# Hybrid decoder step on one Trainium2 core: the upper and lower parts of the weights made by DMAs

## The chip, the cores and the metric

The kernel runs on one core of a Trainium2 chip. The metric is the device time of one execution in microseconds. Five engines with instruction queues of their own share the work: TensorE (PE in the profile), VectorE (DVE), ScalarE (ACT), GpSimd (POOL) and SyncE (SP, which here only issues DMAs). Each engine takes its instructions in the order of its queue and waits on semaphores for the others.

## The reference

One layer of a decoder is applied to 512 prompt rows and 8 sample rows together (520 columns), in float32:

```
z  = RMSNorm(x) @ w_in              # 1024 -> 10240: q k v g | u v | two merge gates
A  = retention(q, k, v), 4 heads, chunks of 128, per-head RMSNorm, silu(g) * o, @ w_ret_o
B  = u * (tril(W_s[g]) @ LN(v) + b[g]), @ w_gm_o
x  = x + (sigmoid(a_ret) * A + sigmoid(a_gm) * B) @ w_o
x  = x + (silu(f_gate) * f_up) @ w_ffn_down      # f = RMSNorm(x) @ w_ffn_in, hidden 2816
y  = RMSNorm(x)
```

Outputs are y for both groups, the retention states of both and the normalised gMLP rows of the samples. Nearly all of the arithmetic is in the six weight matrices.

## The kernel before

**A float32 product in three passes.** Activations lie transposed in SBUF, features on the 128 partitions and the 520 rows as columns, in two halves of 260. A float32 operand is kept as two float32r parts: an upper part, the rounded value, and a lower part, the remainder. A product is upper x upper + upper x lower + lower x upper, summed in PSUM (`product`, L99). One weight block is 128 output features by up to 1024 input features, 512 KB; it gives 8 x 3 x 2 = 48 matmuls of 260 columns.

**Where the weight parts come from.** `weights` (L84) is called once for each block, 180 times in a run: 80 for `w_in`, 16 for `w_ret_o`, 8 each for `w_gm_o` and `w_o`, 44 for `w_ffn_in`, 24 for `w_ffn_down` (8 of them with 768 input features; three are kept for the last tile). SP loads the block into `wraw` (three buffers), ACT copies it to the float32r tile `whi`, which rounds, and DVE subtracts `whi` from `wraw` into `wlo` (`split`, L76). `whi` and `wlo` have two buffers each. The first two blocks come in pieces (`cuts`), so that PE can start on the first piece.

**Stages.** After a start in which x is loaded and split, four heads follow (q, k, v, gate, scores, output, state; the output projection `ps_ro` of a head runs within the next one), then the gMLP branch with the merge gates, then `w_gm_o`, `w_o`, the 44 blocks of the FFN's first matrix and the 24 of its second. In the heads each of 8 samples per head has a state of 512 KB that SP loads (`S`), DVE updates and POOL stores (`out_rss`, L444); POOL also broadcasts the samples' q and k (`qkb`, L436) from a small store in DRAM (`qks`).

**What sets the order.** The program is written in the order of the mathematics; a scheduler of the language reorders the instructions of every engine by its own timeline, and waits follow from the tiles' buffers. POOL does some elementwise work (`sq`, `qf`, `kf`, `gt`, `br`, `gu`, `ms`, `fa`) and issues a few DMAs; its queue, like the others, is in order: an instruction that waits holds up all that stand behind it.

Of the kernel before, what the change touches and what calls it, by code (L numbers as in the profile page):

```python
# [7 lines left out]
F32 = mybir.dt.float32  # L8
F32R = mybir.dt.float32r
I32 = mybir.dt.int32  # L10
AF = mybir.ActivationFunctionType
ALU = mybir.AluOpType

P = 128
# [27 lines left out]
def step_kernel(ctx: ExitStack, tc: tile.TileContext, io):  # L42
    nc = tc.nc

    const = ctx.enter_context(tc.tile_pool(name="const", bufs=1))
    wp = ctx.enter_context(tc.tile_pool(name="wp", bufs=2))
    big = ctx.enter_context(tc.tile_pool(name="big", bufs=NBIG))
    tmp = ctx.enter_context(tc.tile_pool(name="tmp", bufs=NTMP))
    small = ctx.enter_context(tc.tile_pool(name="small", bufs=3))
# [5 lines left out]
    def ttile(name):  # L55
        return tmp.tile([P, T], F32, name=name, tag="tmp")
# [4 lines left out]
    def wide(name, dt=F32):  # L61
        return big.tile([P, 2, T], dt, name=name, tag="big")

    def flat(t):
        return t.rearrange("p a b -> p (a b)")[:, 0:D]
# [10 lines left out]
    def split(hi, lo, src, hi_eng=None, lo_eng=None):  # L76

        if hi_eng is None:
            nc.scalar.copy(out=hi, in_=src)  # L79
        else:  # L80
            hi_eng.tensor_copy(out=hi, in_=src)
        (lo_eng or nc.vector).tensor_tensor(out=lo, in0=src, in1=hi.bitcast(F32), op=ALU.subtract)  # L82

    def weights(src, n, cuts=(), keep=False):  # L84

        raw = wp.tile([P, 8 * P], F32, name="wraw", tag="wraw", bufs=3)
        if keep:
            hi, lo = flat(wide("khi", F32R)), flat(wide("klo", F32R))
        else:
            hi = wp.tile([P, 8 * P], F32R, name="whi", tag="whi")  # L90
            lo = wp.tile([P, 8 * P], F32R, name="wlo", tag="wlo")
        at = [0, *cuts, n]
        for a, b in zip(at, at[1:]):
            sl = slice(a * P, b * P)
            nc.sync.dma_start(out=raw[:, sl], in_=src[:, sl])
            split(hi[:, sl], lo[:, sl], raw[:, sl])
        return hi, lo

    def product(ps, w, at, x, first, last, fs=(0, 1)):  # L99
# [112 lines left out]
    def z_tile(m, name, w=None):  # L212
        w = w or weights(io["w_in"][m], KT)
        ps = acc_psum(name)
        for kt in range(KT):
            product(ps, w, kt, xg[kt], kt == 0, kt == KT - 1)
        return ps
# [7 lines left out]
    rsqrt_table(ones_f)  # L225
    x_load(0)
    w_first = [weights(io["w_in"][0], KT, (2, 4))]
    x_split(0)
    x_load(1)
    x_load(2)  # L230
    x_split(1)
    x_split(2)
    w_first.append(weights(io["w_in"][1], KT, (4,)))
    for kt in range(3, KT):
        x_load(kt)
# [468 lines left out]
    for i in range(KT):  # L704
# [6 lines left out]
        hi = hs[:, i, :]  # L711
# [16 lines left out]
    a = None  # L728
    for i in range(NF):
        a, b = ttile("fa"), ttile("fb")  # L730
# [34 lines left out]
    for i in range(KT - 1):  # L765
        ps = acc_psum("ps_fd")
        down(ps, down_weights(i))
        hi = hs[:, i, :]
# [7 lines left out]
    hi = hs[:, i, :]  # L776
    ps = [aux(f"ps_fd{f}") for f in range(2)]
    blocks = list(down_weights(i, keep=True))
    for f in range(2):
# [5 lines left out]
        if f == 1:  # L785
# [8 lines left out]
            out=hi[:, cols], in0=hi[:, cols], scalar=gains[:, 2, i : i + 1], in1=r, op0=ALU.mult, op1=ALU.mult  # L794
# [5 lines left out]
        for ks in (slice(0, 4), slice(4, 6), slice(6, 8)):  # L800
            nc.sync.dma_start(
                out=io["yT"].rearrange("(k p) t -> p k t", p=P)[:, ks, cols], in_=hs[:, ks, cols]
# [72 lines left out]
```

## Time and profile before

| | |
|---|---|
| time, median of 2 runs | 1162.28 us (1161.21 to 1163.35) |
| profiled execution, its time | 1165.98 us |
| its span, first to last instruction | 1164.2 us |
| PE, PEld busy | 98%, 97% of the span |
| DVE, ACT, POOL busy | 57%, 37%, 18% |
| HBM read, written | 125.02 MB, 21.10 MB |

Busy shares are means over stages; PEld is the load of the stationary operand, which overlaps with PE. The clock that was granted to TensorE is given as a share of 2.4 GHz (1.00 is full speed). DMAs issued from SP stand in the hardware queue, those issued from POOL in the software queue; both use the same 16 DMA engines.

### The profile page before, as it was taken

Reading aid. Unit: us, or ns where it says so; the run is one execution under the profiler, and the core shown is the slowest. Engines: PE = TensorE matmul, PEld = TensorE weight load, DVE = VectorE, ACT = ScalarE, POOL = GpSimd, SP = SyncE. Lnnn points to the kernel's source line nnn. Section 1 sums busy time; section 2 is a strip of 40 time slices with the busy share of each in tenths; the row PEclk is TensorE's granted clock in tenths of the full one; section 3 lists DMA queues with packets and bytes.
Section 4 is the critical chain, followed back from the end, with each engine's and each line's share of the span. In section 5 each row is a group of like instructions: output and inputs, shape, how many; then the busy total and the mean of one; then the engine's idle time right before and its main releaser. Section 6 shows DMA issues by size and latency. Waiting matters only on the chain.

```text
span 1164.2 us, 21641 instructions
## 1 busy us (share of the span) xinstructions
PE 1142.0 (98%) x9242; PEld 1125.6 (97%) x9242; DVE 668.8 (57%) x1040; ACT 435.8 (37%) x672; POOL 209.8 (18%) x175
## 2 busy tenths in 40 slices
PE   8999999999999999999999999999999999999995
PEld 7999999999999998999999999999999999999995
DVE  7788738885787589538434456445545454532233
ACT  4366345433653365323223432343222232322220
POOL 7213201420141013002111222211101010101101
PEclk9999999999999999999999999999999999999998
DMA  7267336633763284222222223422232222223222
GB/s 266 86 217 286 110 110 237 244 109 117 261 212 127 74 276 162 73 91 74 90 74 73 91 91 117 139 94 92 88 106 81 104 90 93 87 90 97 86 78 74
DMA packets 44928, 147.53 MB, mean 127 GB/s; under 512 B 5360, under 2 KB 7808, under 8 KB 44824
## 3 DMA queue, kind: packets, MB, share of 16 engines
q1 hardware_dynamic: 37152, 118.76, 30.2%
q0 software_dynamic: 7680, 27.38, 6.4%
q8 instruction: 73, 1.20, 0.4%
q14 instruction: 23, 0.19, 0.0%
HBM read 125.02 MB, written 21.10 MB: 126 GB/s over the span
## 4 chain that ended last, share of the span: by engine, by line
PE 84%; DVE 7%; DMA 3%; ACT 3%; issue 2%; POOL 0%; DVEq 0%; ACTq 0%; POOLq 0%; SPq 0%
PE ps_fg L105 11%; PE ps_fu L105 11%; PE ps_fd L105 10%; PE ps_ro L105 8%; PE ps_v L105 6%; PE ps_ar L105 4%; PE ps_gm L105 4%; PE ps_g L105 4%; PE ps_gu L105 4%; PE ps_wo L105 4%; PE ps_gv L105 4%; PE ps_ag L105 3%; PE k L105 3%; PE q L105 2%; PE ps_o L460 1%
## 5 line engine op out<-in xcount | busy, mean ns | idle before, releaser
L79 ACT CAST whi<-wraw 128x1024 fp32r<-128x1024 f32 (+2 forms) x180 | 184.8, 1027 | 484.9 <-issue 96.3
L82 DVE TENSOR_TENSOR wlo<-wraw,whi 128x1024 fp32r<-128x1024 f32 (+2 forms) x180 | 256.4, 1425 | 99.2 <-ACT whi L79 94.4
L105 PE MATMUL ps_fg<-hg,whi 128*128 128x260 f32 x704 | 112.5, 282 | 0.0
L105 PE MATMUL ps_fu<-hg,whi 128*128 128x260 f32 x704 | 112.5, 282 | 0.0
L105 PE MATMUL ps_fd<-act,whi 128*128 128x260 f32 x616 | 98.8, 282 | 0.0
L105 PEld LDWEIGHTS ps_fg<-hg,whi 128*128 128x128 f32 x704 | 96.2, 188 | 0.0
L105 PEld LDWEIGHTS ps_fu<-hg,whi 128*128 128x128 f32 x704 | 96.2, 188 | 0.0
L105 PEld LDWEIGHTS ps_fd<-act,whi 128*128 128x128 f32 x616 | 84.4, 188 | 0.0
L105 PE MATMUL ps_g<-xg,whi 128*128 128x260 f32 x512 | 82.7, 283 | 0.0
L105 PE MATMUL ps_ro<-gated,whi 128*128 128x260 f32 x512 | 82.6, 283 | 0.0
L105 PE MATMUL ps_v<-xg,whi 128*128 128x260 f32 x512 | 82.3, 282 | 0.0
L105 PEld LDWEIGHTS ps_ro<-gated,whi 128*128 128x128 f32 x512 | 70.6, 188 | 0.7 <-issue 0.2
L105 PE MATMUL ps_fu<-hg,wlo 128*128 128x260 f32 x352 | 70.8, 282 | 0.0
L105 PE MATMUL ps_fg<-hg,wlo 128*128 128x260 f32 x352 | 70.8, 282 | 0.0
L105 PEld LDWEIGHTS ps_v<-xg,whi 128*128 128x128 f32 x512 | 70.1, 188 | 0.0
L105 PEld LDWEIGHTS ps_g<-xg,whi 128*128 128x128 f32 x512 | 69.9, 188 | 0.0
L746 POOL TENSOR_TENSOR fa<-fa,fb 128x520 f32<-128x520 f32 x22 | 28.8, 1308 | 227.6 <-ACT whi L79 192.8
L442 ACT ACTIVATE kv<-qkb,vs 128x256 f32<-128x256 f32 x128 | 54.1, 498 | 26.9 <-DMA qkb<-qks 23.9
L105 PE MATMUL ps_fd<-act,wlo 128*128 128x260 f32 x308 | 61.8, 282 | 0.0
L745 DVE TENSOR_TENSOR fb<-ps_fu,rstd 128x520 f32<-128x520 f32 x21 | 14.7, 700 | 75.1 <-PE ps_fu L105 75.1
L163 POOL TENSOR_TENSOR sq<-sq,sqr 128x520 f32<-128x520 f32 x19 | 32.9, 1732 | 132.7 <-ACT sqr L161 128.4
L447 DVE SCALAR_TENSOR_TENSOR junk<-S,qkb 128x256 f32<-128x256 f32 x128 | 54.0, 422 | 2.3
(250 smaller groups left out, 2509.3 us busy)
## 6 DMA issues: line engine op xcount, KB each, us to landing
wraw<-in_w_in SPq DMA_DIRECT2D x78, 512.0 KB, 3.5
wraw<-in_w_ffn_in SPq DMA_DIRECT2D x44, 512.0 KB, 3.5
S<-in_st SPq DMA_DIRECT2D x32, 512.0 KB, 4.4
out_rss<-S POOLq DMA_DIRECT2D x32, 512.0 KB, 4.6
qkb<-qks POOLq DMA_DIRECT2D x16, 512.0 KB, 5.0
wraw<-in_w_ret_o SPq DMA_DIRECT2D x16, 512.0 KB, 3.5
wraw<-in_w_ffn_down SPq DMA_DIRECT2D x16, 512.0 KB, 3.5
wraw<-in_w_gm_o SPq DMA_DIRECT2D x8, 512.0 KB, 3.5
```

Of the source, the lines that this page charges most:

```text
L79: nc.scalar.copy(out=hi, in_=src)
L82: (lo_eng or nc.vector).tensor_tensor(out=lo, in0=src, in1=hi.bitcast(F32), op=ALU.subtract)
L105: nc.tensor.matmul((ps[f] if isinstance(ps, list) else ps[:, f])[:, 0:HT], a, x[:, k, f * HT : (f + 1) * HT], start=first and n == 0, stop ...
L163: (add or nc.gpsimd).tensor_tensor(out=acc, in0=acc, in1=q, op=ALU.add)
L442: nc.scalar.activation(out=kv[:, j, :], in_=kb, func=AF.Copy, scale=vs[:, j, b : b + 1])
L447: nc.vector.scalar_tensor_tensor(out=junk, in0=S[:, j, :], scalar=1.0, in1=qb, op0=ALU.mult, op1=ALU.mult, accum_out=os_[:, j, b : b + 1],)
L460: nc.tensor.matmul(ps[:, s * P : NP], vtile(s, l)[:, j * P : (j + 1) * P], score(s, k), start=i == 0, stop=i == 11,)
L745: nc.vector.tensor_tensor(out=halves(b), in0=pu, in1=halves(rstd), op=ALU.mult)
L746: nc.gpsimd.tensor_tensor(out=a, in0=a, in1=b, op=ALU.mult)
```

## The change

`weights` no longer loads a plain copy, except for the first two blocks, which keep the old way with one `wraw` buffer. For the other 178 blocks POOL issues a DMA that writes the block into the float32r tile `whi`, rounding on the way. ACT then writes `-whi` into `wlo`. A second DMA from POOL reads the block from DRAM again and adds it to what stands in `wlo`. `whi` and `wlo` have three buffers each in place of two. Line numbers after this place grow by 7.

```diff
-    wp = ctx.enter_context(tc.tile_pool(name="wp", bufs=2))
+    wp = ctx.enter_context(tc.tile_pool(name="wp", bufs=3))
...
-        raw = wp.tile([P, 8 * P], F32, name="wraw", tag="wraw", bufs=3)
         if keep:
             hi, lo = flat(wide("khi", F32R)), flat(wide("klo", F32R))
         else:
             hi = wp.tile([P, 8 * P], F32R, name="whi", tag="whi")
             lo = wp.tile([P, 8 * P], F32R, name="wlo", tag="wlo")
-        at = [0, *cuts, n]
-        for a, b in zip(at, at[1:]):
-            sl = slice(a * P, b * P)
-            nc.sync.dma_start(out=raw[:, sl], in_=src[:, sl])
-            split(hi[:, sl], lo[:, sl], raw[:, sl])
+        if cuts:
+            raw = wp.tile([P, 8 * P], F32, name="wraw", tag="wraw", bufs=1)
+            at = [0, *cuts, n]
+            for a, b in zip(at, at[1:]):
+                sl = slice(a * P, b * P)
+                nc.sync.dma_start(out=raw[:, sl], in_=src[:, sl])
+                split(hi[:, sl], lo[:, sl], raw[:, sl])
+            return hi, lo
+
+        sl = slice(0, n * P)
+        nc.gpsimd.dma_start(out=hi[:, sl], in_=src[:, sl])
+        nc.scalar.activation(out=lo[:, sl], in_=hi[:, sl].bitcast(F32), func=AF.Copy, scale=-1.0)
+        nc.gpsimd.dma_start(out=lo[:, sl], in_=src[:, sl], accum_op=ALU.add)
         return hi, lo
```

The order of POOL's queue changes in three places. First the start of the program, before the change: squares of x (`sqr`), their sum (`sq`), then the rotary step of head 0.

```order
L159 TENSOR_TENSOR sq<-xt 128x520
L159 TENSOR_TENSOR sqr<-xt 128x520 x2
L163 TENSOR_TENSOR sq<-sq,sqr 128x520
L159 TENSOR_TENSOR sqr<-xt 128x520 x2
L163 TENSOR_TENSOR sq<-sq,sqr 128x520
L159 TENSOR_TENSOR sqr<-xt 128x520
L163 TENSOR_TENSOR sq<-sq,sqr 128x520 x5
L276 TENSOR_TENSOR qf<-rs,rc 128x520
```

And with the change, from the last square on; `whi` is the rounding DMA of a block, `wlo` the adding one.

```order
L166 TENSOR_TENSOR sqr<-xt 128x520
L101 DMA whi<-in_w_in 128x1024 x2
L170 TENSOR_TENSOR sq<-sq,sqr 128x520
L101 DMA whi<-in_w_in 128x1024
L170 TENSOR_TENSOR sq<-sq,sqr 128x520 x2
L103 DMA wlo<-in_w_in 128x1024
L170 TENSOR_TENSOR sq<-sq,sqr 128x520
```

The third block's rounding DMA stands behind the sixth square, and its adding DMA behind three more sums. On ACT its negation stands behind the copy of the second product:

```order
L266 COPY qraw<-q_206 128x520
L168 ACTIVATE sqr<-xt 128x520 x2
L266 COPY qraw<-q_256 128x520
L102 ACTIVATE wlo<-whi 128x1024 x3
L79 CAST sqh<-sq 128x520
```

Second place: POOL in a head (the second one), before. Only the samples' DMAs and elementwise work stand here.

```order
L276 TENSOR_TENSOR kf<-rs,rc 128x520
L275 TENSOR_TENSOR kf<-rc,rs 128x520
L403 DMA qks_199<-row 4x8x128
L436 DMA qkb<-qks_199 128x1024 x2
L444 DMA out_rss<-S 128x1024 x3
L436 DMA qkb<-qks_199 128x1024
L444 DMA out_rss<-S 128x1024
L436 DMA qkb<-qks_199 128x1024
```

With the change, in the same head, from the first stores of states on:

```order
L451 DMA out_rss<-S 128x1024 x2
L101 DMA whi<-in_w_in 128x1024
L103 DMA wlo<-in_w_in 128x1024
L451 DMA out_rss<-S 128x1024
L443 DMA qkb<-qks_199 128x1024
L103 DMA wlo<-in_w_in 128x1024
L451 DMA out_rss<-S 128x1024
L101 DMA whi<-in_w_in 128x1024
L443 DMA qkb<-qks_199 128x1024
L451 DMA out_rss<-S 128x1024 x2
L103 DMA wlo<-in_w_in 128x1024
```

Weight DMAs now stand between the samples' DMAs, behind stores that wait for DVE.

Third place: POOL from `w_gm_o` to the end, before.

```order
L695 TENSOR_TENSOR ms<-ms,br_1929 128x520 x2
L163 TENSOR_TENSOR sq<-sq,sqr 128x520 x6
L746 TENSOR_TENSOR fa<-fa,fb 128x520 x22
L163 TENSOR_TENSOR sq<-sq,sqr 128x520 x6
L799 TENSOR_TENSOR hs<-hs,r_12702 128x260 x3
```

With the change, three blocks in the FFN's first matrix, with what each instruction waits for (DMASW: an earlier DMA of POOL's).

```order
L101 DMA whi<-in_w_ffn_in 128x1024 [waits DMASW2_49,PE_49]
L101 DMA whi<-in_w_ffn_in 128x1024 [waits DMASW3_49,PE_49]
L103 DMA wlo<-in_w_ffn_in 128x1024 [waits DMASW4_49,Activation_49]
L753 TENSOR_TENSOR fa<-fa,fb 128x520 [waits DVE_49,Pool_49]
L103 DMA wlo<-in_w_ffn_in 128x1024 [waits DMASW5_49,Activation_49]
L101 DMA whi<-in_w_ffn_in 128x1024 [waits DMASW6_49,PE_49]
L103 DMA wlo<-in_w_ffn_in 128x1024 [waits DMASW7_49,Activation_49]
```

The rounding DMA of a block waits for PE, which must have finished the block three before it; the adding DMA waits for ACT.

## Rows read from the trace of the kernel before

**Rows 1.** The page's first lines: span, busy time of each engine.

```profile
span 1164.2 us, 21641 instructions
PE 1142.0 (98%) x9242; PEld 1125.6 (97%) x9242; DVE 668.8 (57%) x1040; ACT 435.8 (37%) x672; POOL 209.8 (18%) x175
```

**Rows 2.** Chain that ended last, in order of time: start, length, what.

```profile
217.52 11.46 PE q L105 x96
...
330.08 11.46 PE q L105 x96
...
577.11 2.63 PE ps_mix L631 x24
579.73 11.51 PE ps_ar L105 x96
591.25 11.46 PE ps_ag L105 x96
...
632.80 46.01 PE ps_gu L105 x384
...
817.00 5.73 PE ps_fg L105 x48
822.72 5.73 PE ps_fu L105 x48
```

**Rows 3.** Table by stretch: its length, busy us per engine, granted clock, DMA share, GB/s.

```profile
core 0: us, PE busy (x) PEld busy (x) DVE busy (x) ACT busy (x) POOL busy (x), PEclk, DMA share, GB/s
45.00:128.00 83.00, 82.68 (x646) 80.23 (x645) 72.69 (x147) 43.71 (x82) 25.79 (x24) 1.00 0.57 200
...
217.00:330.00 113.00, 113.00 (x898) 110.61 (x897) 84.28 (x165) 52.76 (x93) 21.59 (x22) 1.00 0.51 179
...
770.00:1023.00 253.00, 253.00 (x2123) 253.00 (x2123) 124.95 (x117) 77.71 (x96) 27.48 (x21) 1.00 0.27 92
```

**Rows 4.** Waits of SP's DMA queue: waiter, releaser, us in total, times, longest.

```profile
SPq L95 <- DVE wlo L82: 777.5, 146, 10.0
```

**Rows 5.** Groups by form: busy us, mean ns of one, idle before and its releasers.

```profile
L82 DVE TENSOR_TENSOR wlo<-wraw,whi 128x1024 fp32r<-128x1024 f32 x168 | 244.9, 1458 | 71.7 <-ACT whi L79 66.9
L79 ACT CAST whi<-wraw 128x1024 fp32r<-128x1024 f32 x168 | 176.3, 1049 | 464.5 <-issue 96.3 <-PE ps_fu L105 86.2 <-PE ps_fg L105 54.7
...
L746 POOL TENSOR_TENSOR fa<-fa,fb 128x520 f32<-128x520 f32 x22 | 28.8, 1308 | 227.6 <-ACT whi L79 192.8 <-ACT fa L742 20.2 <-issue 10.1
L515 POOL TENSOR_TENSOR gt<-gt,of 128x520 f32<-128x520 f32 x16 | 26.6, 1691 | 12.6 <-DVE of L501 12.6
```

**Rows 6.** DMA issues: queue, count, KB each, median us from issue to landing.

```profile
wraw<-in_w_ffn_in SPq DMA_DIRECT2D x44, 512.0 KB, 3.5
out_rss<-S POOLq DMA_DIRECT2D x32, 512.0 KB, 4.6
qkb<-qks POOLq DMA_DIRECT2D x16, 512.0 KB, 5.0
out_rsp<-sf POOLq DMA_DIRECT2D x4, 512.0 KB, 3.2
```

**Rows 7.** Line 444, the states' stores: duration min/median/max, wait before, landing.

```profile
L444 POOL DMA_DIRECT2D out_rss<-S x32: 531/531/538, 73.1 to 440.3; - x32
...
  DVE S L443: 186.8, 32
...
DMA to landing us min/median/max: 2.9/4.6/7.2
```

**Rows 8.** Tile qkb, the samples' broadcasts: landing.

```profile
DMA to landing us min/median/max: 4.0/5.0/6.5
```

**Rows 9.** Timeline of the start: start, length, engine, what.

```profile
16.90 1.51 POOL L159 TENSOR_TENSOR sqr<-xt 128x520 f32<-128x520 f32 x1
...
26.11 0.51 PE L105 MATMUL k<-xg,wlo 128*128 128x260 f32 x2 [0.16 <-DVE wlo L82]
26.22 0.59 ACT L259 COPY qraw<-q 128x520 f32<-128x520 f32 x1
```

## The prediction, made before the changed kernel was run

> **What bounds the kernel now.** I read the busy shares first, then the chain of waits in order of time, then a table by stretch. PE is busy 1142.0 of 1164.2 us [rows 1], so no more than about 22 us can be won by anything that doesn't take matmuls away, and the change takes none. The chain shows the same: from 632.80 us on it is PE without a gap, one weight block after another, 5.73 us each [rows 2]. In a head other matmuls (scores, outputs, transposes, state) stand between the blocks: from one head's q to the next one's it is 112.56 us for 16 blocks, 7.04 us a block [rows 2]. The table says that DVE, which the change relieves, has room everywhere: 125 of 253 us busy in the FFN, 84.3 of 113 in a head [rows 3]. And the weights come early: SP's queue sat 777.5 us, 146 times, until DVE had freed a `wraw` [rows 4]; so loads wait for room and PE doesn't wait for loads. The question is what the new way of making a block costs in delay, with three buffers.
>
> **What goes away.** 178 subtractions on DVE, about 1.46 us each in the 128x1024 form [rows 5], some 250 us of DVE time. I cost this at nothing: PE covers all of it, and the next thing late would still be PE. ACT's rounding copy of 1.05 us [rows 5] becomes a negation of the same shape, taken at the same 1.05 us: nothing on balance, except that it now stands on the path between two DMAs. 178 loads leave SP's queue; the loads of S behind them can start sooner, worth nothing either, as they wait for their own buffers.
>
> **What comes in: a round trip.** Before, a block passed through three raw buffers and two pairs of parts. Now a pair of parts is the only storage. The rounding DMA of block n can't start before PE has finished block n-3; then come landing, negation, the adding DMA, its landing, and the 48 matmuls. So three blocks can't take less than one such round trip. Where PE has only weights to do, three blocks take 3 x 5.73 = 17.2 us; anything above that is stall, a third of it for each block.
>
> For a stretch of weights only (632.80 us to the end, 92 blocks, counted as 90 since 8 are shorter) the trip is:
> - rounding DMA, issue to landing: 4.6. No row shows a rounding DMA. The nearest are POOL's stores of plain 512 KB blocks: 2.9 at the least, 4.6 in the median, 7.2 at the most [rows 7]; SP's load of the same block takes 3.5 [rows 6]. Below 2.9 is excluded: the bytes and the queue are the same.
> - negation 1.05 [rows 5], and 0.3 for waiting its turn on ACT, which is busy 31% here [rows 3].
> - 0.65 for POOL's own queue: one multiplication of 1.31 us for two blocks [rows 5].
> - adding DMA: no row shows one. It must read what the tile holds besides the block, so one pass of 512 KB more than a plain DMA. A pass costs 1.55 us of all 16 DMA engines: share 0.27 of 253 us for 44 blocks [rows 3]. I take 4.6 + 1.55 = 6.15. Its ends are 2.9 (the add hidden in a fastest transfer) and 14.4 (two slowest ones in series).
> - 1.55 for the other DMA that stands right ahead of it in the same queue, as the order shows.
> - matmuls 5.73 [rows 2].
>
> Sum 20.03, a third 6.68, so 0.95 us of stall on each block: 90 x 0.95 = **+85 us**. With the low ends (2.9 + 1.05 + 2.9 + 5.73 = 12.6) there is no stall; with the high ones (7.2 + 1.05 + 0.3 + 0.65 + 14.4 + 1.55 + 5.73 = 30.9) it is 4.6 a block, +411.
>
> The Trainium skill, "DMA: Bandwidth & Descriptors", section on the anatomy of one DMA on the gpsimd path, fits such a DMA as 2.0 us plus its bytes at 436 GB/s; this gives 3.2 us for 512 KB, and by it the trip would be about 14 us, under 17.2, with no stall at all. The trace agrees for the stores of the final states, 3.2 us, and disagrees for the other two kinds, 4.6 and 5.0 [rows 6].
>
> **Heads.** 58 blocks at 7.04 us. The DMA engines are busy 51% there already [rows 3], of which the weights' loads are 16 x 1.55 of 112.56 us, 22%; the adding DMAs, at two passes each, bring 44% more, 95% in all. Landings will therefore be nearer the long ones. With the medians, 5.0 [rows 8] + 1.05 + 0.4 (ACT) + 1.7 (one elementwise step of POOL's ahead [rows 5]) + 6.15 + 1.55 + 5.73 = 21.6, 7.2 a block, +0.15. With the longest, 6.5 [rows 8] and 7.2 + 1.55 [rows 7], 25.7, 8.6 a block, +1.5. The middle is 0.8: **+48 us**.
>
> **gMLP and gates.** 28 blocks; a head begins at 330.08 and lasts 112.56, so this runs from 442.6 to 632.80, 6.79 us a block against 6.68 wanted. Only the gates are tighter: 25.6 us for four blocks with one mixing step [rows 2], 6.4 each; 16 x 0.28 = **+5 us**.
>
> **Start.** The third block's lower part was there at 26.11 [rows 9]. Now its rounding DMA stands behind POOL's sixth square, which ends at 18.41 [rows 9], and lands near 23; but in ACT's order the negation stands behind the copy of the second product, which ends at 26.81 [rows 9]. Then 1.05 and 6.15: 34.0, **+8 us**.
>
> **Sum.** 85 + 48 + 5 + 8 = 146 on the profiled execution's 1165.98, which is 3.7 above the median of the runs: 1312, less the 3.7, 1308. I say **1310 us**.
>
> **Rivals.**
> 1. *Hidden anyway* (ends within 2%). If the adding DMA costs no more than a plain one and nothing queues, the trip is 4.6 + 1.05 + 0.3 + 0.65 + 4.6 + 5.73 = 16.9, just under 17.2. Then only the start remains: 1170. It decides when both landings together stay under 9.4 us. For it: the 3.5 of SP's loads and the 3.2 of POOL's final states [rows 6]. Against it: the medians of the other two kinds, and that adding must read twice. Chance 0.12.
> 2. *The DMA engines become the bound.* If a pass that adds takes four plain passes, 6.2 us, a block needs 7.75 us of all engines. That is +2.02 on 90 blocks, +0.96 on 28, and in the heads, where other traffic takes 29% of 7.04 us, 9.8 a block, +2.75 on 58: 182 + 27 + 160 + 8, and 1539. It decides from 4.2 us for an adding pass. No row speaks for or against the rate of such a pass. Chance 0.18.
> 3. *POOL's queue blocks itself.* The states' stores stood 186.8 us waiting for DVE in POOL's queue [rows 7], at no cost, as nothing urgent was behind them. Now weight DMAs are. If half of that time holds up PE: +93 on top of the forecast, 1401. Chance 0.10.
> 4. *DVE holds up POOL's issuing.* If each issue waited for one DVE step of about 0.7 us, two in a trip, that is 0.47 a block and +83: 1391. Against it: all 32 issues of the stores took 531 to 538 ns [rows 7], in stretches where DVE is busy 75% to 88% [rows 3]. Chance 0.04. The Trainium skill, "SBUF — State Buffer", section on the two separate sides, says that DMAs issued from GpSimd can be starved of descriptors while VectorE runs certain operations; by that these issues should vary, and in this trace they don't.
>
> **Chances.** Forecast 0.55, with a range of its own of 1250 to 1425 (the trip 1 us shorter or 2 us longer on all 176 blocks, 59 or 117 us); rivals 0.12, 0.18, 0.10, 0.04; faster 0.01, for want of anything to win. The range runs from 1185, which leaves out nearly all of rival 1, to 1560, which leaves out the worse half of rival 2, since the high end of the adding DMA lies beyond it. About 2% is what a measurement here can tell from no change; faster by more than that 0.01, within 0.11, slower 0.88.
>
> **What the profile after will show.** Right: PE idle before the first matmul on a `wlo`, released by a DMA, regularly in the FFN; a block near 6.7 us in the chain there; DVE's busy time down by some 250 us at no gain; POOL waiting for ACT between two DMAs; HBM read up by some 90 MB. Rival 1: the chain from 632 us on still PE alone. Rival 2: a DMA share near 1 in the FFN. Rival 3: POOL's waits for the states' DVE step followed by late weights. The forecast would be wrong above all if an adding DMA lands in under 4 or over 9 us; and if the gaps make the granted clock of 1.00 [rows 3] drop, which I have not priced.

## The result, and the profile after

| | before | after |
|---|---|---|
| time, median | 1162.28 us | 1363.37 us (2 runs, 1361.40 to 1365.33) |
| ratio | | 1.173, 95% interval 1.164 to 1.182: slower |
| HBM read | 125.02 MB | 217.29 MB |
| POOL's DMA queue (software) | | 211.95 MB, 64.3% of the 16 engines' span |

The forecast was 1310 us, in a range of 1185 to 1560. The page's first lines, which answer to [rows 1]:

```profile
span 1363.6 us, 21677 instructions
PE 1199.1 (88%) x9242; PEld 1165.7 (85%) x9242; DVE 429.4 (31%) x862; ACT 436.4 (32%) x672; POOL 437.6 (32%) x531
```

DVE lost 239 us of work, and nothing came of it. PE, with the same 9242 matmuls, is busy for 57.1 us more than before and idle for 164.5 us in place of 22.2. These two parts make the 199.4 us by which the span grew.

Where they lie is read from a table with the same columns as [rows 3]. It is cut where the same matmuls begin: the first gMLP product `ps_gv`, the first `ps_gu`, the end. First the kernel before:

```profile
0.00:442.60 442.60, 436.15 (x3400) 424.21 (x3401) 323.93 (x614) 211.46 (x374) 100.66 (x101) 1.00 0.52 184
442.60:632.70 190.10, 186.88 (x1511) 183.26 (x1509) 105.60 (x180) 63.38 (x98) 31.53 (x19) 0.97 0.26 87
632.70:1164.20 531.50, 518.93 (x4333) 518.12 (x4333) 239.23 (x247) 160.97 (x201) 77.62 (x55) 0.99 0.28 93
```

Then the changed kernel, with the FFN's first matrix (44 blocks) once more by itself:

```profile
0.00:515.00 515.00, 453.81 (x3400) 436.48 (x3401) 252.37 (x552) 208.61 (x371) 173.12 (x220) 0.97 0.78 213
515.00:735.00 220.00, 193.52 (x1511) 186.89 (x1509) 76.26 (x153) 63.03 (x97) 65.42 (x76) 0.96 0.63 150
735.00:1363.60 628.60, 551.82 (x4334) 542.35 (x4333) 100.74 (x157) 164.75 (x205) 199.03 (x235) 0.96 0.67 155
902.00:1201.00 299.00, 269.56 (x2115) 266.21 (x2114) 49.70 (x73) 80.19 (x96) 90.67 (x109) 0.95 0.67 154
```

The matmul counts agree row by row, to one, so the rows may be subtracted: start and heads 72 us longer, gMLP and gates 30, weights only 97. A block of the FFN's first matrix takes 299 / 44 = 6.80 us where [rows 2] had 5.73. The DMA engines, at 0.67 in the mean, are not full.

What PE waited for stands in the view of the tile `wlo` (idle time in us, times):

```profile
  DMA wlo<-in_w_in: 73.8, 34
  DMA wlo<-in_w_ffn_in: 29.4, 16
  DMA wlo<-in_w_ffn_down: 15.3, 9
  DMA wlo<-in_w_ret_o: 12.9, 10
  DMA wlo<-in_w_gm_o: 8.0, 4
  DMA wlo<-in_w_o: 4.0, 3
```

The sum, 143.4 us, is all of the additional idle time (142.3): PE waits for adding DMAs and for nothing else that is new.

One round trip in the timeline of the FFN (start, length, engine, what, idle before):

```profile
1026.35 0.84 POOL L103 DMA_DIRECT2D wlo<-in_w_ffn_in  x1 [7.10 <-ACT wlo L102]
...
1027.78 0.55 POOL L101 DMA_DIRECT2D whi<-in_w_ffn_in  x1 [0.58 <-PE ps_fu L112]
...
1033.55 0.56 POOL L101 DMA_DIRECT2D whi<-in_w_ffn_in  x1 [3.65 <-PE ps_fg L112]
...
1034.22 1.06 ACT L102 ACTIVATE wlo<-whi 128x1024 fp32r<-128x1024 f32 x1 [3.66 <-DMA whi<-in_w_ffn_in]
...
1035.59 0.88 POOL L103 DMA_DIRECT2D wlo<-in_w_ffn_in  x1 [1.48 <-ACT wlo L102]
...
1037.31 1.06 ACT L102 ACTIVATE wlo<-whi 128x1024 fp32r<-128x1024 f32 x1 [1.50 <-DMA whi<-in_w_ffn_in]
...
1040.92 0.51 PE L112 MATMUL ps_fg<-hg,wlo 128*128 128x260 f32 x2 [1.22 <-DMA wlo<-in_w_ffn_in]
```

PE finishes a `ps_fu` block and frees its pair; the rounding DMA goes out at 1027.78 and has landed when ACT negates at 1034.22, 6.4 us later; the adding DMA goes out at 1035.59, and PE gets the lower part at 1040.92, 1.22 us late. The first row shows POOL itself waiting 7.10 us for ACT at the head of its queue. The rounding DMA right behind that adding DMA took 6.4 us; the one at 1033.55, issued 7.2 us after the last adding DMA, landed in 3.7.

What POOL waited for, in the whole run (waiter, releaser, us, times, longest):

```profile
POOL wlo L103 <- ACT wlo L102: 512.5, 131, 10.4
...
POOL out_rss L451 <- DVE S L450: 59.3, 23, 5.9
```

The wait named by the POOL-queue rival, the states' stores for DVE, shrank from 186.8 [rows 7] to 59.3; another one, 512.5 us for negations, took its place.

Last, the price that the forecast left out. After a wait of 2.14 us that ended at 1020.70, the table by stretch shows the granted clock (third number from the end):

```profile
1012.00:1018.00 6.00, 6.00 (x52) 6.00 (x51) 0.70 (x1) 2.56 (x3) 2.96 (x4) 1.00 0.62 165
1020.70:1023.70 3.00, 3.00 (x14) 3.00 (x15) 0.00 (x0) 0.00 (x0) 0.00 (x0) 0.50 1.05 262
```

Before the wait it is 1.00 (2.4 GHz), and for the 3.0 us after it 0.50 (1.2 GHz).

### The profile page after: what moved, and what is told of

Same layout as the page of the kernel before. It is cut to its first block, busy times and chain, and to the rows that moved or that the text cites. A ratio compares the mean times of both kernels' runs of the same rounds, so it can differ in the third digit from the quotient of the medians.

```text
span 1363.6 us, 21677 instructions
## 1 busy us (share of the span) xinstructions
PE 1199.1 (88%) x9242; PEld 1165.7 (85%) x9242; DVE 429.4 (31%) x862; ACT 436.4 (32%) x672; POOL 437.6 (32%) x531
## 3 DMA queue, kind: packets, MB, share of 16 engines
q0 software_dynamic: 58944, 211.95, 64.3%
HBM read 217.29 MB, written 21.10 MB: 175 GB/s over the span
## 4 chain that ended last, share of the span: by engine, by line
issue 39%; PE 21%; DMA 20%; POOL 14%; DVE 3%; ACT 2%; POOLq 0%; SPq 0%; DVEq 0%; ACTq 0%
PE ps_v L112 5%; DMA wlo<-in_w_in 5%; POOL wlo L103 4%; POOL whi L101 4%; DMA whi<-in_w_ffn_down 3%; PE ps_fu L112 3%; PE ps_ro L112 2%; DMA whi<-in_w_in 2%; DMA wlo<-in_w_ret_o 2%; PE q L112 2%; DMA wlo<-in_w_ffn_in 2%; DMA qks<-row 2%; POOL fa L753 2%; PE ps_fd L112 1%; PE ps_gu L112 1%
## 5 line engine op out<-in xcount | busy, mean ns | idle before, releaser
L102 ACT ACTIVATE wlo<-whi 128x1024 fp32r<-128x1024 f32 (+1 forms) x175 | 183.8, 1051 | 612.0 <-DMA whi<-in_w_in 207.4
L103 POOL DMA_DIRECT2D wlo<-in_w_in x78 | 69.9, 900 | 274.9 <-ACT wlo L102 225.0
L112 PE MATMUL ps_fu<-hg,whi 128*128 128x260 f32 x704 | 119.0, 293 | 0.0
L112 PEld LDWEIGHTS ps_fu<-hg,whi 128*128 128x128 f32 x704 | 102.8, 200 | 0.0
L112 PE MATMUL ps_fu<-hg,wlo 128*128 128x260 f32 x352 | 75.6, 298 | 15.8 <-DMA wlo<-in_w_ffn_in 15.8
L103 POOL DMA_DIRECT2D wlo<-in_w_ffn_in x44 | 38.8, 881 | 147.1 <-ACT wlo L102 135.7
L112 PEld LDWEIGHTS ps_fu<-hg,wlo 128*128 128x128 f32 x352 | 57.9, 202 | 17.5 <-DMA wlo<-in_w_ffn_in 17.5
L101 POOL DMA_DIRECT2D whi<-in_w_in x78 | 56.2, 721 | 51.6 <-PE q L112 15.4
L112 PEld LDWEIGHTS ps_fg<-hg,wlo 128*128 128x128 f32 x352 | 55.3, 192 | 15.3 <-DMA wlo<-in_w_ffn_in 15.2
L112 PE MATMUL ps_ro<-gated,wlo 128*128 128x260 f32 x256 | 53.2, 290 | 12.9 <-DMA wlo<-in_w_ret_o 12.9
```

What stands on the lines that cost most here:

```text
L101: nc.gpsimd.dma_start(out=hi[:, sl], in_=src[:, sl])
L102: nc.scalar.activation(out=lo[:, sl], in_=hi[:, sl].bitcast(F32), func=AF.Copy, scale=-1.0)
L103: nc.gpsimd.dma_start(out=lo[:, sl], in_=src[:, sl], accum_op=ALU.add)
L112: nc.tensor.matmul((ps[f] if isinstance(ps, list) else ps[:, f])[:, 0:HT], a, x[:, k, f * HT : (f + 1) * HT], start=first and n == 0, stop ...
```

## Experiments

Theory: **the buffers' round trip**. Three pairs of parts allow three blocks for each trip of rounding DMA, negation, adding DMA and matmuls, and the trip is longer than three blocks' matmuls. Rivals: the DMA engines are the bound, since each block now takes a rounding and an adding pass; POOL's in-order queue is the bound, since a rounding DMA stands behind an adding DMA that waits for a negation; adding is dear by itself, or rounding is.

**Four upper parts.** `whi` gets a fourth buffer, for which the start's raw copy moves to another pool; the same DMAs, the same order rules.

```diff
-            hi = wp.tile([P, 8 * P], F32R, name="whi", tag="whi")
+            hi = wp.tile([P, 8 * P], F32R, name="whi", tag="whi", bufs=4)
...
-            raw = wp.tile([P, 8 * P], F32, name="wraw", tag="wraw", bufs=1)
+            raw = flat(wide("wraw"))
```

> Change kept, but the upper part has four buffers instead of three (the start's raw copy moves into the big pool to make room); the same DMAs, bytes and passes. Round-trip theory (a block waits for rounding DMA 6.2 us, negation 1.05, adding DMA 5.4 and hand-offs before PE can use it, three blocks per trip, 20.4 us with its matmuls): a trip now serves four blocks, 20.4 / 4 = 5.1 us, less than the 5.73 us of matmuls, so the stalls in the weights-only stretch vanish and 1175 to 1210 us remain (start and part of the heads). Rival, DMA engines or DRAM as the bound: the same passes, within 2% of 1363. Rival, POOL's in-order queue: adding DMAs still stand behind waiting instructions, above 1300.

Measured: 1202.13 us, ratio to before 1.029 (1.025 to 1.034). Its FFN in the table by stretch:

```profile
800.00:1055.00 255.00, 255.00 (x2120) 255.00 (x2119) 50.26 (x73) 77.32 (x95) 89.42 (x109) 1.00 0.86 182
```

PE is busy without a gap at clock 1.00, with the same DMAs per block at a DMA share of 0.86. One buffer gives back 161 of the 201 us, so neither the number of passes nor the price of adding bounds the changed kernel. POOL's waits for negations fall from 512.5 to 109.5 us: with a fourth buffer the scheduler also put rounding and adding DMAs in turn, so this run alone doesn't part the trip from POOL's queue. Of the 35 us that its span is still longer, 29 lie in the start and heads (`ps_gv` begins at 471.7) and 7 in the weights only.

**Two pairs.** The pool `wp` with `bufs=2` in place of 3.

> Change kept, with two buffers for each part. Round-trip theory: 20.4 us for two blocks, 10.2 each, if the landings stay the same; somewhat less, as fewer DMAs queue behind each other: 1750 to 1950 us. DMA-bound rival: the passes are the same, 1363 to 1400.

Measured: 1721.3 us, a little below the range, far from what a bound by the DMA engines gives. The FFN takes 1503.7 - 1103.9 = 399.8 us, 9.09 a block, so two blocks take 18.2 and, in the changed kernel, three take 20.4. The trip stays nearly the same while the number of blocks in it changes. It is 2.2 us shorter with two pairs: in the FFN rounding DMAs landed in 4.1 us in the median here, in 6.1 there, what is left for hand-offs is 1.0 shorter, and the matmuls are 0.8 a block longer (6.9 for 6.13).

**Lower part last.** With three pairs, PE does the 32 matmuls on the upper part first and the 16 on the lower part after them (`chain`, used for all blocks but the first two). 28 more matmuls stand ahead of the first on the lower part, 3.3 us at [rows 2]'s 5.73 for 48.

```diff
+    def chain(ps, w, xs, n, at=0, fs=(0, 1)):
+
+        for part in (0, 1):
+            for k in range(n):
+                sl = slice((at + k) * P, (at + k + 1) * P)
+                for m in ((0, 1) if part == 0 else (0,)):
+                    for f in fs:
+                        nc.tensor.matmul(
+                            ps[:, f][:, 0:HT], w[part][:, sl], xs[k][:, m, f * HT : (f + 1) * HT],
...
-        for kt in range(KT):
-            product(ps, w, kt, hg[kt], kt == 0, kt == KT - 1)
+        chain(ps, w, hg, KT)
```

> Change kept with three buffers, but in each block PE does the 32 matmuls on the upper part first and the 16 on the lower part last, instead of 4 and 2 in turn. Round-trip theory: the adding DMA is needed some 28 matmuls or 3.3 us later, so the trip is 17.1 us for three blocks, 5.7 each, just what the matmuls take: 1180 to 1235 us, with what is left in the heads, where the output projection's blocks are used in halves. DMA-bound rival: no gain, within 2% of 1363. POOL-queue rival: part of the gain, 1270 to 1320.

Measured: 1315.61 us, ratio 1.128 (1.122 to 1.134): a miss for the buffers' trip taken as the only cause, inside what the POOL-queue rival gave. POOL's timeline in the FFN:

```profile
999.32 0.88 POOL L103 DMA_DIRECT2D wlo<-in_w_ffn_in  x1 [0.33 <-issue]
999.90 0.88 POOL L101 DMA_DIRECT2D whi<-in_w_ffn_in  x1
1008.01 0.84 POOL L103 DMA_DIRECT2D wlo<-in_w_ffn_in  x1 [7.23 <-ACT wlo L102]
1008.56 0.86 POOL L101 DMA_DIRECT2D whi<-in_w_ffn_in  x1
...
1010.38 0.87 POOL L101 DMA_DIRECT2D whi<-in_w_ffn_in  x1
1016.57 0.89 POOL L103 DMA_DIRECT2D wlo<-in_w_ffn_in  x1 [5.32 <-ACT wlo L102]
1018.74 0.87 POOL L103 DMA_DIRECT2D wlo<-in_w_ffn_in  x1 [1.28 <-ACT wlo L102]
1019.28 0.89 POOL L101 DMA_DIRECT2D whi<-in_w_ffn_in  x1
```

POOL issues a rounding DMA, then stands 7.23 us at the adding DMA of that same block until it has landed and been negated; only then can the next rounding DMA go out, and it waits for no PE then: its buffer is free already. Three blocks take 19.4 us of this (999.90 to 1019.28), against 17.2 of matmuls and 20.4 before the edit. So there are two limits close together, and lifting the first shows the second.

**Lower part last, rounding one block ahead.** An order without a semaphore is added: a block's adding DMA stands behind the next block's rounding DMA in POOL's queue.

```diff
+    adds = []
...
-        nc.gpsimd.dma_start(out=hi[:, sl], in_=src[:, sl])
+        up = nc.gpsimd.dma_start(out=hi[:, sl], in_=src[:, sl])
+        if adds and not keep:
+            tc.add_manual_dep(
+                adds[-1].ins, up.ins.name,
+                mybir.DependencyInfo(mybir.DependencyClass.NoSync, mybir.DependencyReason.DATA),
+            )
...
-        nc.gpsimd.dma_start(out=lo[:, sl], in_=src[:, sl], accum_op=ALU.add)
+        adds.append(nc.gpsimd.dma_start(out=lo[:, sl], in_=src[:, sl], accum_op=ALU.add))
```

> As e2 (three buffers, lower part last), and the issue order on POOL is fixed so that the rounding DMA of the next block always stands ahead of the adding DMA of this one. In e2 the expected 1180 to 1235 us became 1316. If POOL's in-order queue is what is left there (in e2 it waits twice, some 8 us each, for every three blocks, 19 us where the matmuls take 17.2), the strict one-ahead order takes that away and the time falls to 1175 to 1225 us. If the DMA engines or the buffers are what is left in e2, the order changes nothing: within 2% of 1316.

Measured: 1194.75 us, ratio 1.026 (1.021 to 1.030). POOL's timeline in the FFN now (the multiplication between them left out):

```profile
1002.97 0.55 POOL L103 DMA_DIRECT2D whi<-in_w_ffn_in  x1 [3.74 <-PE ps_fu L131]
1003.80 0.86 POOL L110 DMA_DIRECT2D wlo<-in_w_ffn_in  x1 [0.28 <-ACT wlo L109]
...
1008.72 0.57 POOL L103 DMA_DIRECT2D whi<-in_w_ffn_in  x1 [1.65 <-PE ps_fg L131]
1009.69 0.87 POOL L110 DMA_DIRECT2D wlo<-in_w_ffn_in  x1 [0.39 <-ACT wlo L109]
```

A rounding DMA leaves every 5.75 us, released by PE, and the adding DMA waits 0.3 to 0.4 us. Here the slow side waits for PE, which is how a kernel bound by PE looks. The buffers are three pairs still, and every block still has its adding DMA.

**The order alone**, without the later lower part.

> The change with the one-ahead order on POOL alone; three buffers and the matmuls' order as in the change. Round-trip theory: the trip of 20.4 us for three blocks is set by the buffers and stays: 1330 to 1370 us. POOL-queue theory as the sole cause of the change's loss: 1180 to 1230.

Measured: 1366.99 us, ratio 1.176 (1.168 to 1.184), the same as the changed kernel. Rounding DMAs land sooner (4.5 us in the median in place of 6.2), the adding ones later (7.4 in place of 5.4): the order only moves the queueing from one to the other, and the trip stays. POOL's queue is therefore not the cause by itself. One stage does gain: from the first `ps_gv` to the first `ps_gu` it takes 205.7 us in place of 220.1, while start and heads take 8 and the weights only 5 longer. Either edit alone leaves over 1300 us; both together reach 1195.

**Adding alone.** The upper part comes from a plain load by SP and a copy on ACT, the adding DMA stays.

```diff
-        nc.gpsimd.dma_start(out=hi[:, sl], in_=src[:, sl])
+        raw = wp.tile([P, 8 * P], F32, name="wraw", tag="wraw", bufs=1)
+        nc.sync.dma_start(out=raw[:, sl], in_=src[:, sl])
+        nc.scalar.copy(out=hi[:, sl], in_=raw[:, sl])
```

> One part of the change alone: the adding DMA stays (with ACT's negation), but the upper part is made as before from a plain load by SP into one raw buffer and a rounding copy on ACT. DMA passes per block as with the change. Round-trip theory: the load runs ahead, the trip is copy 1.05, negation 1.05, adding DMA 5.4, hand-offs 1 and 5.73 of matmuls, 14.2 us for three blocks, 4.7 each: no stall, 1165 to 1200 us. DMA-bound rival: within 2% of 1363.

Measured: 1196.48 us in its one run. With the adding DMA on every block, and its FFN at 250 us of PE in 250 us, adding isn't what the changed kernel loses by. What shortens the trip, as I read it, is that `wraw` takes the load before a pair is free; that wasn't tried apart.

**Rounding alone.** The rounding DMA stays; SP loads the plain copy as well, and DVE subtracts as before.

> The other part of the change alone: the rounding DMA stays (three upper buffers), but the lower part is made as before by DVE from a plain copy that SP loads (two raw, two lower buffers). Round-trip theory: landing about 4 us, subtraction 1.2, hand-offs 1 and 5.73 of matmuls, 12 us for three blocks, 4 each: no stall, 1165 to 1190 us. If rounding by DMA is itself what costs: above 1250.

Measured: 1176.54 us in its one run; the rounding DMAs landed in 3.3 / 3.8 / 10.8 us (least, median, most). Without a second DMA that depends on the first, the kernel is some 13 us from the one before (1163.69 in the same comparison), 9 of them ahead of the first `ps_gv` (451.9).

**No adding.** The second DMA copies in place of adding.

```diff
-        nc.gpsimd.dma_start(out=lo[:, sl], in_=src[:, sl], accum_op=ALU.add)
+        nc.gpsimd.dma_start(out=lo[:, sl], in_=src[:, sl])
```

> The change, but the second DMA copies (and rounds) the block into the lower part instead of adding it to what stands there: the add is left out, everything else, with ACT's negation, stays. If adding costs one more pass through the DMA engines, this DMA lands about 1 us sooner, and the rounding DMA that queues behind it as well: the trip falls from 20.4 to about 18.3 us, 6.1 a block, 1200 to 1270 us. If adding costs no more than copying: within 2% of 1363.

Measured: 1204.2 us in its one run. The landings of the second DMA, here and in the changed kernel:

```profile
DMA to landing us min/median/max: 3.4/3.9/9.6
```

```profile
DMA to landing us min/median/max: 4.7/5.4/10.6
```

Adding costs 1.3 to 1.5 us of landing. Without it the rounding DMAs land sooner too (4.5 in the median in place of 6.2), and the trip nearly fits: in the FFN a block takes 5.96 us (796.2 to 1058.5 for 44). The engines' time agrees. With a rounding and a plain pass per block (rounding alone), the share is 0.60 of 250 us over 43.6 blocks, 3.4 us; with a plain and an adding pass (adding alone) it is 0.84, 4.8. With a plain pass at 1.55 [rows 3] the rounding one takes 1.9 and the adding one 3.3. In the changed kernel a block takes 0.67 x 299 / 44 = 4.6, which leaves 2.7 for adding. So an adding pass takes 2.7 to 3.3, some two plain ones.

**The order of matmuls, by itself**, in the kernel before.

> The kernel before, its weights made as before, with only the order of the matmuls that the lower-last kernels use. It tells what the order is worth by itself. If it is worth nothing without a late lower part: 1158 to 1172, PE busy 1138 to 1146 us. If the order costs or saves PE time by itself (fewer changes of the stationary operand in a row, other gaps): outside 1150 to 1180, and then the results of the two lower-last kernels carry that as well.

Measured: 1165.39 us, ratio 0.999 (0.997 to 1.001). Nothing, so the two lower-last kernels may be read as they stand.

**States' stores on SP**, on the kernel with both edits.

```diff
-            nc.gpsimd.dma_start(out=io["rss"][b, h].rearrange("p (j d) -> p j d", j=NC), in_=S)
+            nc.sync.dma_start(out=io["rss"][b, h].rearrange("p (j d) -> p j d", j=NC), in_=S)
```

> The kernel with the lower part last and the rounding DMA one block ahead (1194.75 us), with the 32 stores of the samples' states issued from SP in place of POOL. In that kernel some 20 of its 30 us over the kernel before lie ahead of the first gMLP product. If they come from POOL's queue, in which weight DMAs stand behind stores that wait for DVE (the POOL-queue rival): 1174 to 1186. If they come from the DMA engines, busy 0.89 of the time in the heads with the same bytes either way: 1188 to 1202.

Measured: 1187.71 us, ratio 1.018 (1.014 to 1.021), between the two ranges. The medians differ by 7 us. In the two profiled executions 4 us come off by the first `ps_gv` (463.2 to 459.3), but as much again between `ps_gv` and `ps_gu` (191.3 to 186.9), where this edit changes nothing, so the 4 us are not shown to be its own. From 45 to 460 us POOL's largest waits were, with the stores on POOL,

```profile
POOL out_rss L471 <- DVE S L470: 80.6, 26, 9.0
POOL whi L103 <- PE ps_v L131: 39.7, 9, 6.1
```

and with the stores on SP,

```profile
POOL whi L103 <- PE ps_g L131: 52.4, 15, 7.0
POOL qkb L463 <- DVE junk L474: 45.4, 8, 8.8
```

One wait for DVE went, another, of the samples' broadcasts, grew from 17.3 to 45.4. So the POOL-queue rival, with this wait, holds for 4 us here at the most; the other 17 us of the heads and start remain, with the DMA engines at 0.9 from 120 to 460 us. How much of them is the engines' share wasn't taken apart.

**And the start made as before**, for the third to the sixth block.

> The same as the store-on-SP kernel, and the third to the sixth block made as before (load by SP, rounding copy, subtraction on DVE), which takes two reads less for four blocks out of the start. PE sat about 12 us idle between 0 and 120 us in the kernel it builds on, against 6 before. Expected 4 to 9 us below the store-on-SP kernel; if the start is hidden by what follows: the same within 2 us. Above the kernel before in any case, since nothing here takes PE work away: 1164 or more.

Measured: 1192.55 us, ratio 1.021 (1.018 to 1.024), a miss: no gain, if anything a loss of 5 us. The third block's lower part is there sooner (first used at 30.9 in place of 33.7), but its upper part comes later (26.9 in place of 24.9), and the next head's q starts at 109.4 in place of 105.5. Why the head gives it back is open.

No variant of the change beat the kernel before. Those that came nearest keep PE busy without a gap in the FFN and lose in the start and the heads.

## Why the prediction was right, and where its sizes were off

The direction and the mechanism held: a round trip through three pairs of parts took the place of work on DVE that PE had covered. The signs it named are there: late `wlo` before PE, POOL waiting for ACT, DVE down by 239 us at no gain, 92 MB more read. One sign of being wrong came too, the drop of the granted clock (0.95 in the FFN), and the forecast stood all the same. The terms of the sum:

| term | forecast | measured | PE idle longer | PE busy longer |
|---|---|---|---|---|
| start and heads | 8 + 48 | 72 | 55 | 18 |
| gMLP and gates | 5 | 30 | 23 | 7 |
| weights only | 85 | 97 | 64 | 33 |
| sum | 146 | 199 | 142 | 57 |

(The two right columns come from the two tables by stretch: length less PE's busy time, and busy time.)

**Weights only.** The forecast had 20.03 us for three blocks, 14.30 of them outside the matmuls. Measured in the FFN: 20.4, of which the matmuls take 269.56 / 44 = 6.13, and 14.3 are left. The terms inside that moved against each other. The rounding DMA landed in 6.1 us in the median where 4.6 was taken, the adding one in 5.4 where it was 7.7: the wait behind the neighbouring DMA fell on the other one of the two. The hand-offs, which are what remains, took 1.7 in place of 0.95. The landings were taken 0.8 too long together, the hand-offs 0.75 and the matmuls 0.40 too short; the balance, a third of some 0.36 us on each of 90 blocks, is about the 12 us by which the term was short. That it came so near is luck in part.

The matmuls took longer for two reasons. The mean granted clock of 0.95 over 299 us is worth at most 15 us, 0.34 a block. And a wait breaks the overlap of matmuls: behind the one at 1040.92 two took 0.51 us, where an unbroken run ends two every 0.24 (5.73 for 48), some 4 us for the 16 waits here. The prediction named the clock and put no price on it. What the clock adds to the time stays open: in the FFN of the kernel with the order alone it was 0.99, and a block took 300.3 / 44 = 6.83 us all the same.

```profile
897.80:1198.10 300.30, 264.06 (x2118) 257.60 (x2117) 49.16 (x73) 77.75 (x95) 92.20 (x109) 0.99 0.72 154
```

**gMLP and gates** was the worst term. The step that failed is that the trip there would be no longer than in the FFN, at 6.68 a block. It was 220 / 28 = 7.86, so 23.6 for three. Landings there were like those of the FFN (medians 6.2 and 5.3), the matmuls took 6.9, so 4 us and not 1 went to hand-offs. POOL's wait from 515 to 735 us and a piece of its timeline in the gates show which:

```profile
POOL wlo L103 <- ACT wlo L102: 101.3, 21, 8.0
```

```profile
658.71 0.89 POOL L103 DMA_DIRECT2D wlo<-in_w_in  x1 [5.75 <-ACT wlo L102]
659.29 0.88 POOL L101 DMA_DIRECT2D whi<-in_w_in  x1
...
667.13 0.88 POOL L103 DMA_DIRECT2D wlo<-in_w_in  x1 [5.62 <-ACT wlo L102]
668.90 0.57 POOL L101 DMA_DIRECT2D whi<-in_w_in  x1 [0.90 <-issue]
675.26 0.85 POOL L103 DMA_DIRECT2D wlo<-in_w_in  x1 [5.78 <-ACT wlo L102]
675.82 0.85 POOL L101 DMA_DIRECT2D whi<-in_w_in  x1
```

The rounding DMAs at 659.29 and 675.82 wait for no PE: their pairs were free, and POOL stood at the adding DMA of the block before. Two blocks take 16.5 us so, 8.3 each: a landing, a negation and the issues of one block after the other, however many pairs there are. Here POOL's queue is the limit, for which the forecast had 0.65 us in a trip; with the order alone the rounding DMAs wait for PE there (130 us in four rows of POOL's waits), and the stage is 14 us shorter.

**Start and heads.** The start's number is right, the third block's lower part came at 33.50 with 34.0 forecast, but two misses cancel in it: the negation began at 25.50 where 26.81 was taken, and the adding DMA went out only at 28.21, behind POOL's sums, to land 5.3 us later where 6.15 was taken. In the heads the landings' sum was 6.8 + 5.9 = 12.7 in the medians; with the medians the forecast had 5.0 + 7.7, the same, and from them a stall of 0.15 us. It chose a middle value of 0.8 us of stall for each of the 58 blocks; PE's additional idle time, 55 less 7 for the start, is 0.8 a block too. This agreement is luck as far as the runs show: what lengthens the trip in the heads beyond these landings was not taken apart. The 18 us of longer matmuls come on top.

**Rivals.** *Hidden anyway* fell with the landings, 11.5 us together where 9.4 was its limit. The Trainium skill, "DMA: Bandwidth & Descriptors", in its section on the anatomy of one DMA, fits a DMA on the gpsimd path as 2.0 us plus its bytes at 436 GB/s, an estimate of 3.2 us for 512 KB. The trace agrees for the quickest rounding DMAs (3.3); their median was 3.8 where they were the only weight DMAs of POOL's queue, and 6.1 with two in the queue. *The DMA engines* decide from 4.2 us for an adding pass; it takes 2.7 to 3.3, and the kernel with four upper parts ran the same passes without a gap. *POOL's queue* was given the wrong wait (stores for DVE) and too low a rank: by another wait, its own negations, it is the next limit in the FFN, 1 us per three blocks under the first, and in the gates the first. *DVE holding up POOL's issuing*: rounding DMAs in the FFN do take 538 to 1138 ns to issue, but with the order alone they take 546 to 579, with DVE busy 17% and 16% there, so this goes with the order in the queue and not with DVE.

## What to carry to other kernels

Work that lies beside a full engine is free, and taking it away buys nothing; what the replacement adds in latency is paid as soon as one trip through the buffers exceeds what the engine does with the blocks in them, so work out that trip, with the queueing, before the busy shares. Two DMAs that depend on each other through a third engine, in one in-order queue, need the next block's first DMA ahead of this block's second, and room or time for it: either edit alone left over 1300 us here, both gave 1195. When a bound engine gets gaps, its clock and its restarts lengthen its work as well, 57 us of it here beside 142 us of gaps.

## What was not expected of the hardware

- An adding DMA of 512 KB takes about two plain passes of the DMA engines (2.7 to 3.3 us against 1.55), lands in 4.7 us at the least against 3.3, and keeps POOL 0.87 us in issuing against 0.53 for a copying DMA to the same tile.
- Rounding to float32r in a DMA cost little that the landings show: 3.3 us at the least and 3.8 in the median, where SP's plain load took 3.5 in the median [rows 6].
- A wait of 2.14 us was followed by a granted clock of 0.50 for 3.0 us. In all PE was busy 57 us longer on the same matmuls, 0.4 us for each us of additional waiting. The mean granted clock, 0.961 over 1363.6 us in place of 0.990 over 1164.2, is worth at most 41 of it; the restarts, at 0.27 us for each of 76 waits, some 20.
